# Lane pauses, layer-norm leads and one buffer ring in a hybrid encoder layer

## The chip, the cores and the metric

The kernel runs on one core of a Trainium2 chip. The metric is the device time of one execution in microseconds (us). Beside it stands the profiled execution, from which every duration below is taken: its span runs from the first instruction to the last.

The engines are named as in the profile: PE multiplies matrices, PEld loads its weights, DVE and ACT do elementwise work, POOL issues some transfers (DMAs), SP issues most of them. Each engine takes its instructions strictly in the order of the program.

## The reference

Two token sequences go through the same layer: a prompt of 512 tokens and a sample of 1024, both 2048 wide, in float32.

```
h    = rms_norm(x, norm_g)
z    = h @ w_in                      # 2048 -> conv value, GLU, gate, q, k, v, gate
conv = silu(layer_norm(depthwise31(val * sigmoid(glu)))) @ w_pw * silu(c_gate)
attn = banded_sink_attention(rope(q), rope(k), v) * silu(a_gate)   # 8 heads, 2 kv heads
y    = rms_norm(x + concat(conv, attn) @ w_out, final_norm_g)
```

The convolution is 1024 channels wide, with 31 taps. Attention goes by blocks of 128 queries, each over up to three blocks of 128 keys, with a sink logit for each head. The layer norm is over the 1024 convolution channels of one token.

## The kernel before

**Products.** Every operand of a large product is split into a high part (rounded by ACT) and a low part (the rest, by DVE); three matmuls, high by high, high by low and low by high, make one product. The sample's projections go through a Strassen-like scheme of seven products in place of eight (class Unit): a unit is a pair of output columns by half of the depth, seven products of 12 matmuls each, 84 in all. Weight sums are made by DVE (make1: `t2` is the second of them, the operand of product P6), token sums are loaded as they are wanted. The prompt's projection by w_in is plain: 44 jobs of 48 matmuls.

**Stages, in PE's order.** The sample's units on w_in; the prompt's 44 jobs; then the upper half of the depth of w_out for the sample (8 units), w_pw (4 units, class Gated), the lower half of w_out (8 units), and at the end the prompt's w_pw and w_out. Between two stages with other token sums stands a switch: the old stage's last unit and the new stage's first bring in the new sums, 4 tiles at a time (load_sum, token_sum). On the switch from w_pw to w_out's lower half the first two units run side by side, product by product: unit 0 in the PSUM banks a, b, c and unit 1 in s, s, pt. These two are of class Total.

**Lanes.** Everything that isn't a large product is written as generators in three lanes: attn, conv (the taps on DVE) and prep. After every three matmuls the main loop adds their nominal time times the lane's rate to its credit, and a lane with credit takes its next step. A generator says `yield n` to be left alone until n of credit is earned. So a yield divided by the rate is a distance on PE. The list of steps thus found goes through a scheduler that places every instruction in its engine's queue; what stands in the queues at the end is fixed when the program is built.

- `attention(g, b, k, v)` is one block of four heads: query parts, pause S1, scores (L1239) for two heads, pause S6, two more, pause S6, exponentials (L1253), S2, scaling by the reciprocal (L1258, L1260), S4, then for each key block transposes (L1273), parts, S5 and the product with V (L1268, bank pv).
- `group(g)` makes the parts of K and V and then runs the blocks. For the prompt these parts lie in the f ring of 7 buffers, which the taps, the sums and the layer norm share.
- The attn lane has rate 1.8 (RUSH) while the sample's attention starts, 2.2 from the prompt's job 18 on (prepare), and 2.0 (LATE) once `attention_sums` has multiplied the sample's attention by its gate and stored its sums. attention_sums goes in four steps j: load the heads (L1370 from att_d, L1371 from ag_d), pause, multiply (L1375), sums (L1354 to L1357) into the u and g rings, store. The prompt's two groups follow it in the lane.
- `Post.prepare` is the layer norm of one half of the sample's tokens, in the prep lane at rate 1.0: sums over channels, their spread over partitions by a product with ones (`sums`, L781), squares (L1616 to L1618), column sums (L769), reciprocal root (L787 to L792), diagonal matrices (`spread`, L805) and their product with ones (L810), then scaling. Between the operands and the product with ones stands a lead of S8 = 6000. LastPost is the same for the prompt, much later.

**Rings.** A tag is a ring of buffers; a new tile waits until an old one of its ring is read. Rings that matter here: a (4 buffers of 1024 columns: query parts, probability parts, wide token sums, gated attention), p (4 of 512: probabilities, narrow token sums), g and u (4 each of 512: PSUM copies and sums to be stored), f (7 of 1024).

**SP** issues loads and stores in the order of its queue, and a load that waits holds all behind it.

In class Unit the buffer of `t2` is chosen by these lines:

```
if self.late:
    t2 = self.e.G([HALF, P]) if self.side or not self.total else self.e.A([HALF, P], F32)
else:
    t2 = self.e.PT("p", NP, [HALF, P])
```

Of the kernel before, what the change touches and what calls it, by code (L numbers as in the profile page):

```python
# [22 lines left out]
NB = 4  # L23
# [70 lines left out]
class Unit:  # L94
# [34 lines left out]
    late = False  # L129
# [141 lines left out]
class Onto(Unit):  # L271


    late = True
# [38 lines left out]
class Gated(Unit):  # L313


    late = True
# [36 lines left out]
class Total(Unit):  # L353


    late = True
    next = None

    def __init__(self, e, w, cols, k, source, part, done):
# [137 lines left out]
class Encoder:  # L497
# [273 lines left out]
        nc.vector.tensor_scalar(v, ps[:, 0:b], mul, add, ALU.mult, ALU.add)  # L771
        return v

    def sums(self, x):

        hi, lo = self.U(dt=F32R), self.U(dt=F32R)
        self.parts(hi, lo, x)
        yield S8
        ps = self.PS("s", [W])
        for n, part in enumerate((hi, lo)):  # L780
            self.nc.tensor.matmul(ps, self.ones_r, part, start=n == 0, stop=n == 1)  # L781
        return ps
# [8 lines left out]
        nc.vector.tensor_scalar(t, t, -0.5, 1.5, ALU.mult, ALU.add)  # L791
        nc.vector.tensor_tensor(out, s, t, ALU.mult)  # L792

    def spread(self, cols, b=NB, room=None):

        nc = self.nc
        hi = self.work.tile([P, b], F32R, tag="tinyr", bufs=4, name=self.name("tinyr"))
        lo = self.small(b)
        nc.vector.tensor_copy(hi, cols)
        nc.vector.tensor_tensor(lo, cols, hi.bitcast(F32), ALU.subtract)  # L800
        parts = []
        for part in (hi.bitcast(F32), lo):
            dg = (room or self.U)([b * P], F32R)
            for j in range(b):
                nc.vector.tensor_scalar(dg[:, j * P : (j + 1) * P], self.ident, part[:, j : j + 1], None, ALU.mult)  # L805
            parts.append(dg)
        yield S8
        ps = self.PS("s", [b * P])
        for n, dg in enumerate(parts):
            nc.tensor.matmul(ps, self.ones_r, dg, start=n == 0, stop=n == 1)  # L810
        return ps


class Sequence:
# [407 lines left out]
    def attention(self, g, b, k, v):  # L1222

        e, nc, B = self.e, self.e.nc, self.B
        lo, hi = max(b - 1, 0), min(b + 2, B)
        n = (hi - lo) * P
        keys = slice(lo * P, hi * P)
        mask = e.mask[:, (lo - b + 1) * P : (hi - b + 1) * P]
        qs = e.A([2, GROUP, P])
        with e.tc.high_priority(SOON):  # L1230
            e.parts(qs[:, 0], qs[:, 1], self.q)
        self.load_query(g, b + 1)
        m, nm, es, l, r = (e.small(GROUP) for _ in range(5))
        yield S1
        pr = []
        for h in range(GROUP):
            ps = e.PS("s", [3 * P])
            for p, (x, y) in enumerate(((0, 0), (0, 1), (1, 0))):
                nc.tensor.matmul(ps[:, 0:n], qs[:, x, h], k[y][:, keys], start=p == 0, stop=p == 2)  # L1239
            p = e.PT("p", NP, [W])  # L1240
            with e.tc.high_priority(SOON):
                nc.vector.tensor_tensor_reduce(
                    p[:, 0:n], ps[:, 0:n], mask, SCALE, e.sink[:, g * GROUP + h : g * GROUP + h + 1],
                    ALU.add, ALU.max, accum_out=m[:, h : h + 1],
                )
            pr.append(p)
            if h % 2:
                yield S6
        with e.tc.high_priority(SOON):
            nc.vector.tensor_scalar(nm, m, -1.0, None, ALU.mult)  # L1250
            nc.vector.tensor_tensor(es, e.sink[:, g * GROUP : (g + 1) * GROUP], m, ALU.subtract)  # L1251
            for h, p in enumerate(pr):
                nc.scalar.activation(p[:, 0:n], p[:, 0:n], AF.Exp, bias=nm[:, h : h + 1], accum_out=l[:, h : h + 1])  # L1253
            nc.scalar.activation(es, es, AF.Exp)
        yield S2
        with e.tc.high_priority(SOON):
            nc.vector.tensor_tensor(l, l, es, ALU.add)
            nc.vector.reciprocal(r, l)  # L1258
            for h, p in enumerate(pr):
                nc.scalar.activation(p[:, 0:n], p[:, 0:n], AF.Identity, scale=r[:, h : h + 1])  # L1260
        yield S4
        pv = e.PS("pv", [GROUP, P])
        last = hi - lo - 1

        def products(i, pt):
            vs = slice((lo + i) * P, (lo + i + 1) * P)
            for p, (x, y) in enumerate(((0, 0), (0, 1), (1, 0))):
                nc.tensor.matmul(pv, v[x][:, vs], pt[:, y], start=i == 0 and p == 0, stop=i == last and p == 2)  # L1268

        for i in range(hi - lo):  # L1270
            tp = e.PS("pt", [GROUP, P])
            for h, p in enumerate(pr):
                nc.tensor.transpose(tp[:, h], p[:, i * P : (i + 1) * P], e.ident)  # L1273
            pt = e.A([2, GROUP, P])
            with e.tc.high_priority(SOON):
                e.parts(pt[:, 0], pt[:, 1], tp)
            yield S5
            products(i, pt)
        o = e.U([GROUP, P])
        with e.tc.high_priority(SOON):  # L1280
# [53 lines left out]
class Mix:  # L1334
# [26 lines left out]
    def attention_sums(self, then):  # L1361

        e, nc, seq = self.e, self.e.nc, self.seq
        for j in range(HALF):
            if j == HALF - 1:
                then()
            x = []
            for h in (j, j + HALF):
                f, g = e.A([TS], F32), e.F([TS])
                nc.sync.dma_start(f, seq.att_d[h // GROUP][:, h % GROUP, :])  # L1370
                nc.sync.dma_start(g, seq.ag_d[h])  # L1371
                x.append((h, f, g))
            yield e.attn.rate * 1.5 * LEAD
            for h, f, g in x:
                nc.vector.tensor_tensor(f, f, g, ALU.mult)  # L1375
                e.store(self.xT[NC + h], f)
                yield 1500
            self.block_sums(1, j, x[0][1], x[1][1])
            self.gated += 1
            yield 4000  # L1380
        e.attn.rate = LATE
# [197 lines left out]
class Post:  # L1579


    N = 512

    def __init__(self, e, seq, t0, out):
        self.e, self.seq, self.t0, self.out = e, seq, t0, out
# [2 lines left out]
    def prepare(self):  # L1588
        e, nc, seq, t0, N = self.e, self.e.nc, self.seq, self.t0, self.N
        cols = slice(t0, t0 + N)  # L1590
        bc, vs = self.room(), self.room()
        mu, rs, va = bc[:, 0], bc[:, 1], vs[:, 0]
        sq = (bc[:, 1], vs[:, 1])
        pairs = []
        for i in range(0, NC, 2):
            t = self.room()
            for j in (0, 1):
                nc.sync.dma_start(t[:, j], seq.conv_d[i + j][:, cols])
            pairs.append(t)
        xc = [pairs[i // 2][:, i % 2] for i in range(NC)]  # L1600
        both = lambda row: row.unsqueeze(1).broadcast_to([P, 2, N])
        yield 2 * LOAD
        nc.vector.tensor_tensor(vs, pairs[0], pairs[1], ALU.add)
        for t in pairs[2:]:
            nc.vector.tensor_tensor(vs, vs, t, ALU.add)
            yield 1500
        nc.vector.tensor_tensor(va, va, vs[:, 1], ALU.add)
        yield S3
        ps = yield from e.sums(va)
        nc.scalar.activation(mu, ps, AF.Copy, scale=1.0 / C)  # L1610
        yield 1000
        for i, t in enumerate(pairs):
            nc.vector.tensor_tensor(t, t, both(mu), ALU.subtract)
            for j in (0, 1):
                n = 2 * i + j
                nc.scalar.activation(sq[j] if n else va, t[:, j], AF.Square)  # L1616
                if n:
                    nc.vector.tensor_tensor(va, va, sq[j], ALU.add)  # L1618
            yield 2500
        yield S3  # L1620
        v = yield from e.column_sums(va, N, 1.0 / C, LN_EPS)
        r = e.small(NB)
        e.rsqrt(r, v, NB)
        yield S7
        ps = yield from e.spread(r)
# [12 lines left out]

# [21 lines left out]
class LastPost(Post):  # L1660


    PAIRS = (2, 3, 0, 1)
    HT = TP // 2

    def __init__(self, e, seq, t0, out, sums):
        super().__init__(e, seq, t0, out)
# [39 lines left out]
    def combine(self, m, x1, x2):  # L1707

        e, nc, h = self.e, self.e.nc, self.HT

# [584 lines left out]
```

## Time and profile before

| | |
|---|---|
| time, median of 3 | 2079.45 us (2077.16 to 2080.08) |
| the profiled execution's own time | 2082.61 us |
| its span | 2080.8 us |
| TensorE clock granted, mean | 0.997 |
| DVE busy | 1754.9 us (84%) |
| ACT busy | 1096.5 us (53%) |
| DMA, mean over the span | 237 GB/s |

A row of the groups of instructions or of the timeline names the line, the engine, the operation and the tiles written and read; "idle before" is how long that engine did nothing just ahead of it, with what ended the wait. PEclk is the TensorE clock that was granted, 1.00 at full speed. Matmul counts given below as places on PE are counts of the product matmuls of 512 columns (the projections' own) from the program's start; there are 8316.

### The profile page before, as it was taken

Reading aid. Unit: us, or ns where it says so; the run is one execution under the profiler, and the core shown is the slowest. Engines: PE = TensorE matmul, PEld = TensorE weight load, DVE = VectorE, ACT = ScalarE, POOL = GpSimd, SP = SyncE. Lnnn points to the kernel's source line nnn. Section 1 sums busy time; section 2 is a strip of 40 time slices with the busy share of each in tenths; the row PEclk is TensorE's granted clock in tenths of the full one; section 3 lists DMA queues with packets and bytes.
Section 4 is the critical chain, followed back from the end, with each engine's and each line's share of the span. In section 5 each row is a group of like instructions: output and inputs, shape, how many; then the busy total and the mean of one; then the engine's idle time right before and its main releaser. Section 6 shows DMA issues by size and latency. Waiting matters only on the chain.

```text
span 2080.8 us, 27254 instructions
## 1 busy us (share of the span) xinstructions
PE 2054.6 (99%) x9208; PEld 1685.7 (81%) x9208; DVE 1754.9 (84%) x2895; ACT 1096.5 (53%) x1811; POOL 160.8 (8%) x240
## 2 busy tenths in 40 slices
PE   9999999999999999999999999999999999999998
PEld 7888888888887888788888887878778887888886
DVE  8767899998899899879766888688998887998887
ACT  7485445333465555645555775358541544454554
POOL 0111111111111111100000000000001002100000
PEclk9999999999999999999999999999999999999999
DMA  8888886854577767854555567886899778778897
GB/s 288 309 300 256 197 218 227 300 205 153 194 240 194 179 168 180 276 166 157 162 184 175 162 204 246 305 281 220 254 306 345 242 256 247 243 255 287 287 329 278
DMA packets 245405, 492.99 MB, mean 237 GB/s; under 512 B 23952, under 2 KB 84752, under 8 KB 245264
## 3 DMA queue, kind: packets, MB, share of 16 engines
q1 hardware_dynamic: 218944, 427.26, 61.7%
q0 software_dynamic: 25024, 61.88, 12.5%
q10 hardware_dynamic: 1296, 2.11, 0.3%
q8 instruction: 72, 1.18, 0.2%
q14 instruction: 69, 0.57, 0.1%
HBM read 328.89 MB, written 162.27 MB: 236 GB/s over the span
## 4 chain that ended last, share of the span: by engine, by line
PE 72%; DMA 8%; DVE 8%; issue 7%; ACT 3%; POOL 1%; SPq 0%; ACTq 0%; POOLq 0%; DVEq 0%
PE a L207 22%; PE c L207 11%; PE a L736 10%; PE b L207 5%; PE b L736 5%; PE c L736 5%; PE a L1959 2%; PE pv L1268 2%; PE s L1239 2%; PE s L207 2%; DVE hl L577 1%; PE s L1959 1%; PE pt L1273 1%; DMA f<-ag_d 1%; DVE f L1073 1%
## 5 line engine op out<-in xcount | busy, mean ns | idle before, releaser
L207 PE MATMUL a<-t,hl 128*128 128x512 f32 x2832 | 683.0, 391 | 5.2 <-ACT hl L576 2.5
L207 PEld LDWEIGHTS a<-t,hl 128*128 128x128 f32 x2832 | 530.6, 188 | 118.7 <-ACT hl L576 3.3
L577 DVE TENSOR_TENSOR hl<-raw,hl 128x1024 fp32r<-128x1024 f32 (+3 forms) x334 | 333.8, 1000 | 147.4 <-ACT hl L576 146.0
L576 ACT ACTIVATE hl<-raw 128x1024 fp32r<-128x1024 f32 (+3 forms) x334 | 293.4, 879 | 296.9 <-PE c L207 83.8
L207 PE MATMUL c<-t,hl 128*128 128x512 f32 x1416 | 343.1, 390 | 1.3 <-ACT t L576 1.3
L207 PEld LDWEIGHTS c<-t,hl 128*128 128x128 f32 x1416 | 265.6, 188 | 57.0 <-ACT t L576 1.8
L736 PE MATMUL a<-t,hl 128*128 128x512 f32 x1152 | 287.0, 396 | 0.0
L736 PEld LDWEIGHTS a<-t,hl 128*128 128x128 f32 x1152 | 213.3, 189 | 42.4
L1110 DVE SCALAR_TENSOR_TENSOR f<-f,c_w_dw,f 128x512 f32<-128x512 f32 x248 | 173.1, 747 | 0.2
L207 PE MATMUL b<-t,hl 128*128 128x512 f32 x708 | 171.8, 390 | 0.0
L1073 DVE SCALAR_TENSOR_TENSOR f<-f,c_w_dw,f 128x512 f32<-128x512 f32 x232 | 162.6, 744 | 2.3 <-ACT f L1068 2.3
L207 PEld LDWEIGHTS b<-t,hl 128*128 128x128 f32 x708 | 132.6, 188 | 27.7 <-DVE t L577 0.4
L736 PE MATMUL c<-t,hl 128*128 128x512 f32 x576 | 143.5, 395 | 0.4 <-DVE hl L577 0.4
L736 PE MATMUL b<-t,hl 128*128 128x512 f32 x576 | 139.6, 393 | 1.8 <-DVE t L581 0.8
L736 PEld LDWEIGHTS b<-t,hl 128*128 128x128 f32 x576 | 106.8, 188 | 25.2 <-DVE t L581 1.1
L736 PEld LDWEIGHTS c<-t,hl 128*128 128x128 f32 x576 | 106.1, 188 | 21.7 <-DVE hl L577 0.8
L236 ACT ACTIVATE u<-a 128x512 f32<-128x512 f32 x89 | 53.0, 595 | 91.9 <-PE a L207 86.0
L236 ACT ACTIVATE g<-a 128x512 f32<-128x512 f32 x87 | 51.9, 596 | 89.2 <-PE a L207 81.3
L1102 DVE SCALAR_TENSOR_TENSOR f<-f,w_both,f 128x512 f32<-128x512 f32 x120 | 89.8, 749 | 2.0
L1253 ACT ACTIVATE p<-p,tiny 128x384 f32<-128x384 f32 (+1 forms) x96 | 54.6, 570 | 55.3 <-DVE tiny L1251 31.7
L576 ACT ACTIVATE a<-pt 128x512 fp32r<-128x512 f32 x64 | 37.9, 592 | 58.1 <-PE pt L1273 58.0
L577 DVE TENSOR_TENSOR a<-pt,a 128x512 fp32r<-128x512 f32 x64 | 43.9, 686 | 27.1 <-ACT a L576 26.8
(360 smaller groups left out, 2791.9 us busy)
## 6 DMA issues: line engine op xcount, KB each, us to landing
raw<-w_in SPq DMA_DIRECT2D x170, 512.0 KB, 5.2
raw<-w_out SPq DMA_DIRECT2D x31, 512.0 KB, 5.2
wsum_P<-raw SPq DMA_DIRECT2D x47, 256.0 KB, 3.5
raw<-wsum_P SPq DMA_DIRECT2D x18, 512.0 KB, 4.9
f<-x_s SPq DMA_DIRECT2D x16, 512.0 KB, 8.4
raw<-w_pw SPq DMA_DIRECT2D x16, 512.0 KB, 4.9
g<-wsum_P SPq DMA_DIRECT2D x28, 256.0 KB, 4.8
a<-sum_S SPq DMA_DIRECT2D x24, 256.0 KB, 6.2
```

The source lines that it names most:

```text
L207: nc.tensor.matmul(acc, hl[:, l, o, j, :], toks[j][:, r], start=name in FRESH and j == 0 and q == 0, stop=name in LAST and j == HALF - 1 a ...
L236: nc.scalar.activation(t, bank, AF.Copy)
L576: nc.scalar.activation(hi, x, AF.Copy)
L577: nc.vector.tensor_tensor(lo, x, hi.bitcast(F32), ALU.subtract)
L736: nc.tensor.matmul(job.acc[0], hl[:, l, kk // HALF, kk % HALF, :], r, start=i == 0 and p == 0, stop=i == nk - 1 and p == 2,)
L1073: nc.vector.scalar_tensor_tensor(t, h[:, j : j + T], w(j), t, ALU.mult, ALU.add)
L1102: nc.vector.scalar_tensor_tensor(m0, odd[:, j : j + H], both(j), m0, ALU.mult, ALU.add)
L1110: nc.vector.scalar_tensor_tensor(out, d[:, j : j + H], w(2 * j + k), out if j else m0, ALU.mult, ALU.add)
L1239: nc.tensor.matmul(ps[:, 0:n], qs[:, x, h], k[y][:, keys], start=p == 0, stop=p == 2)
L1253: nc.scalar.activation(p[:, 0:n], p[:, 0:n], AF.Exp, bias=nm[:, h : h + 1], accum_out=l[:, h : h + 1])
L1268: nc.tensor.matmul(pv, v[x][:, vs], pt[:, y], start=i == 0 and p == 0, stop=i == last and p == 2)
L1959: nc.tensor.matmul(acc[t], self.toks[name, m][:, x, i, t * P : (t + 1) * P], parts[i][l].rearrange("p a b -> p (a b)"), start=fresh and fi ...
```

## The change

Three things are edited.

1. In an attention block the pauses S6 and S4 are multiplied by `hurry`, the lane's rate over 1.8 and at least 1. At rate 2.2 that is 1.22, at 2.0 it is 1.11, at 1.8 nothing changes. The pause ahead of each multiplication of attention_sums grows from 1.5 to 2 times 9000 times the rate.
2. The layer norm of the sample's two halves gets 12000 in place of 6000 between operands and product with ones, at both places. The prompt's keeps 6000.
3. Class Total is no longer `late`: `t2` of the two switch units comes from the p ring. Before, unit 0's came from the a ring and unit 1's, which runs at the side, from the g ring.

```
 class Total(Unit):
-    late = True
     next = None
...
-    def sums(self, x):
+    def sums(self, x, lead=S8):
...
-        yield S8
+        yield lead
...
-    def spread(self, cols, b=NB, room=None):
+    def spread(self, cols, b=NB, room=None, lead=S8):
...
-        yield S8
+        yield lead
...
         m, nm, es, l, r = (e.small(GROUP) for _ in range(5))
+        hurry = max(1, e.attn.rate / RUSH)
         yield S1
...
             if h % 2:
-                yield S6
+                yield S6 * hurry
...
-        yield S4
+        yield S4 * hurry
         pv = e.PS("pv", [GROUP, P])
...
-            yield e.attn.rate * 1.5 * LEAD
+            yield e.attn.rate * 2 * LEAD
             for h, f, g in x:
                 nc.vector.tensor_tensor(f, f, g, ALU.mult)
...
 class Post:
     N = 512
+    lead = 2 * S8
...
-        ps = yield from e.sums(va)
+        ps = yield from e.sums(va, self.lead)
...
-        ps = yield from e.spread(r)
+        ps = yield from e.spread(r, lead=self.lead)
...
 class LastPost(Post):
     HT = TP // 2
+    lead = S8
```

No instruction of PE is added or taken away. From the middle of the sample's attention (place 4602) to the end of the prompt's, the queues of all engines are rearranged; the prompt's first scores move from place 5542 to 5631, its last product with V from 6159 to 6303. In the changed program lines between 358 and 1232 have numbers lower by one.

**DVE, the layer norm of the sample's second half.** Before, the rows from the reciprocal root (L788 to L792, tiles tiny) on; a_11176 and a_11180 are the first two heads of attention_sums, t_ tiles are the layer norm's. The diagonals L805 follow eight rows behind the last row shown.

```order
L788 RECIPROCAL tiny_11253<-tiny_11253 128x4
L1375 TENSOR_TENSOR a_11176<-a_11176,f_11177 128x1024
L789 TENSOR_TENSOR tiny_11254<-tiny_11253 128x4
L1073 SCALAR_TENSOR_TENSOR f_11109<-f_10957,c_w_dw,f_11109 128x512
L790 TENSOR_TENSOR tiny_11254<-tiny_11254,tiny_11250 128x4
L1375 TENSOR_TENSOR a_11180<-a_11180,f_11181 128x1024
L577 TENSOR_TENSOR hl_11360<-raw_11239,hl_11360 128x1024
L791 TENSOR_SCALAR tiny_11254<-tiny_11254 128x4
L1354 TENSOR_TENSOR u_11304<-a_11176,a_11180 128x512
L792 TENSOR_TENSOR tiny_11252<-tiny_11253,tiny_11254 128x4
```

With the change the same two multiplications (now of a_11221 and a_11225) stand among the sums of squares (L1619, into t_1493_10780), which PE's column sums read:

```order
L1375 TENSOR_TENSOR a_11221<-a_11221,f_11222 128x1024
L1619 TENSOR_TENSOR t_1493_10780<-t_1493_10780,t_1492_10779 128x512
L1375 TENSOR_TENSOR a_11225<-a_11225,f_11226 128x1024
L576 TENSOR_TENSOR hl_11306<-raw_11210,hl_11306 128x1024
L1619 TENSOR_TENSOR t_1493_10780<-t_1493_10780 128x512
L1072 SCALAR_TENSOR_TENSOR f_11054<-f_10925,c_w_dw,f_11054 128x512 x2
L1614 TENSOR_TENSOR t_1497_10790<-t_1497_10790,t_1492_10779 128x1024
L1072 SCALAR_TENSOR_TENSOR f_11054<-f_10925,c_w_dw,f_11054 128x512 x5
L1619 TENSOR_TENSOR t_1493_10780<-t_1493_10780,t_1492_10779 128x512
```

The multiplications moved from the far side of the column sums to the near side, twelve rows ahead of the first row that reads the column sums.

**DVE, the switch from w_pw to w_out.** Here a_15149 is t2 of unit 0, hl_15156 the parts made of it, t_ tiles are token parts. Before:

```order
L577 TENSOR_TENSOR t_2186_15064<-p_14967,t_2186_15064 128x512
L577 TENSOR_TENSOR t_2191_15089<-a_15005,t_2191_15089 128x512
L577 TENSOR_TENSOR t_2192_15092<-a_15005,t_2192_15092 128x512
L577 TENSOR_TENSOR t_2216_15221<-g_15076,t_2216_15221 128x512
L143 TENSOR_TENSOR a_15149<-raw_14985,raw_14882 128x512
L577 TENSOR_TENSOR t_2193_15095<-a_15006,t_2193_15095 128x512
L143 TENSOR_TENSOR raw_14882<-raw_14882,a_15149 128x512
L577 TENSOR_TENSOR hl_15156<-a_15149,hl_15156 128x512
```

With the change, p_15149 is t2 of unit 0 and p_15185 that of unit 1 (it was g_15185, 22 rows ahead of a_15149):

```order
L576 TENSOR_TENSOR t_2186_15064<-p_14967,t_2186_15064 128x512
L576 TENSOR_TENSOR t_2191_15089<-a_15005,t_2191_15089 128x512
L143 TENSOR_TENSOR p_15149<-raw_14985,raw_14882 128x512
L576 TENSOR_TENSOR t_2201_15134<-f_15132,t_2201_15134 128x512
L143 TENSOR_TENSOR raw_14882<-raw_14882,p_15149 128x512
L576 TENSOR_TENSOR t_2202_15139<-u_14940,t_2202_15139 128x512
L576 TENSOR_TENSOR t_2203_15142<-f_14971,t_2203_15142 128x512
L576 TENSOR_TENSOR hl_15156<-p_15149,hl_15156 128x512
L576 TENSOR_TENSOR t_2204_15146<-g_15014,t_2204_15146 128x512
L143 TENSOR_TENSOR p_15185<-f_15047,raw_14945 128x512
L257 TENSOR_TENSOR g_15210<-s_15224,g_15210 128x512
L143 TENSOR_TENSOR raw_14945<-raw_14945,p_15185 128x512
```

Unit 0's t2 is made nine rows earlier and unit 1's twenty rows later. p_15185 takes the buffer of p_15149 and waits until that tile's store to memory has landed. On PE, P6 of unit 0 now stands ahead of P6 of unit 1; before it stood behind it.

**ACT, K and V parts of the prompt's second group.** Before, K's part (f_12761) stood by itself, with V's (f_12762) eleven rows behind it:

```order
L576 ACTIVATE a_12920<-u_12767 128x512
L576 ACTIVATE t_1831_12850<-f_12805 128x512
L576 ACTIVATE hl_12976<-raw_12878 128x1024
L576 ACTIVATE f_12761<-a_12763 128x512
L576 ACTIVATE t_1854_12958<-f_12853 128x512
L576 ACTIVATE t_1855_12961<-f_12853 128x512
```

With the change both (f_13063, f_13064) stand together, and V's waits for the store of the taps' result (f_12420), whose buffer it takes:

```order
L575 ACTIVATE hl_13313<-raw_13156 128x1024
L575 ACTIVATE f_13063<-a_13065 128x512
L575 ACTIVATE f_13064<-a_13067 128x512
L575 ACTIVATE a_13179<-u_13069 128x512
L1067 ACTIVATE f_13195<-f_12998,c_b_dw,c_w_dw 128x512
L1068 ACTIVATE f_13195<-f_12998,c_w_dw 128x512
L575 ACTIVATE hl_13376<-raw_13156 128x512
```

They moved from the loading of the upper half's token sums (t_ tiles) into the units of w_out; weights for a unit (hl_13376) stand behind them.

More of the change, by code (lines that the diff above doesn't have):

```diff
@@ L353 @@
 class Total(Unit):
-    late = True
     next = None
@@ L772, in column_sums, with sums @@
         return v
-    def sums(self, x):
+    def sums(self, x, lead=S8):
         hi, lo = self.U(dt=F32R), self.U(dt=F32R)
         self.parts(hi, lo, x)
-        yield S8
+        yield lead
         ps = self.PS("s", [W])
@@ L792, in rsqrt, with spread @@
         nc.vector.tensor_tensor(out, s, t, ALU.mult)
-    def spread(self, cols, b=NB, room=None):
+    def spread(self, cols, b=NB, room=None, lead=S8):
         nc = self.nc
@@ L806, in spread @@
             parts.append(dg)
-        yield S8
+        yield lead
         ps = self.PS("s", [b * P])
@@ L1233, in attention @@
         m, nm, es, l, r = (e.small(GROUP) for _ in range(5))
+        hurry = max(1, e.attn.rate / RUSH)
         yield S1
@@ L1247, in attention @@
             if h % 2:
-                yield S6
+                yield S6 * hurry
         with e.tc.high_priority(SOON):
@@ L1260, in attention @@
                 nc.scalar.activation(p[:, 0:n], p[:, 0:n], AF.Identity, scale=r[:, h : h + 1])
-        yield S4
+        yield S4 * hurry
         pv = e.PS("pv", [GROUP, P])
@@ L1372, in attention_sums @@
                 x.append((h, f, g))
-            yield e.attn.rate * 1.5 * LEAD
+            yield e.attn.rate * 2 * LEAD
             for h, f, g in x:
@@ L1582 @@
     N = 512
+    lead = 2 * S8
     def __init__(self, e, seq, t0, out):
@@ L1608, in prepare @@
         yield S3
-        ps = yield from e.sums(va)
+        ps = yield from e.sums(va, self.lead)
         nc.scalar.activation(mu, ps, AF.Copy, scale=1.0 / C)
@@ L1624, in prepare @@
         yield S7
-        ps = yield from e.spread(r)
+        ps = yield from e.spread(r, lead=self.lead)
         nc.scalar.activation(rs, ps, AF.Copy)
@@ L1664 @@
     HT = TP // 2
+    lead = S8
     def __init__(self, e, seq, t0, out, sums):
```

## The prediction

> **What bounds the kernel now.** I read the page's first part first, then PE's waits, then windows round the longest of them.
>
> ```profile
> PE 2054.6 (99%) x9208; PEld 1685.7 (81%) x9208; DVE 1754.9 (84%) x2895; ACT 1096.5 (53%) x1811; POOL 160.8 (8%) x240
> ```
>
> PE sets the time. Of the span of 2080.8 us it is idle for 26.2, in the whole program. The change leaves PE's work as it is, so it can win only two things: idle time, and clock that idle time costs. PE's waits, grouped by the waiting line and its releaser (us in total, times, longest):
>
> ```profile
> PE s L810 <- DVE u L805: 2.5, 2, 2.3
> PE a L207 <- ACT hl L576: 2.5, 2, 2.0
> PE s L1239 <- ACT f L576: 1.5, 1, 1.5
> PE c L207 <- ACT t L576: 1.3, 1, 1.3
> PE a L207 <- DVE tiny L1258: 1.0, 1, 1.0
> ```
>
> The three longest belong to the three things that are edited: the layer norm's spread (L810), the switch's P6 (L207 on hl) and the prompt's first scores (L1239). Windows of 4 us behind each, and two long stretches (busy us and count of PE, PEld, DVE, ACT, POOL, then granted clock, DMA share, GB/s):
>
> ```profile
> 1294.00:1298.00 4.00, 3.63 (x10) 2.87 (x11) 4.00 (x11) 0.60 (x1) 0.00 (x0) 0.57 1.03 413
> 1374.00:1378.00 4.00, 3.02 (x18) 2.52 (x19) 3.92 (x10) 3.67 (x5) 0.00 (x0) 1.00 0.97 362
> 1436.00:1600.00 164.00, 162.01 (x749) 131.16 (x748) 156.85 (x282) 77.43 (x150) 14.83 (x27) 1.00 0.88 292
> 1734.00:1738.00 4.00, 3.78 (x11) 3.04 (x11) 4.00 (x7) 0.66 (x2) 0.00 (x0) 0.57 0.91 246
> 2000.00:2081.00 81.00, 70.65 (x311) 57.85 (x309) 59.30 (x110) 38.87 (x70) 0.00 (x0) 0.97 0.84 294
> ```
>
> Behind the first and third waits (2.32 and 2.00 us, below) the granted clock is 0.57; behind the second, of 1.5 us, it stays at 1.00. So a wait of 2 us or more costs a second time: 0.43 of 3.63 us is 1.6 us at the first, 0.43 of 3.78 is 1.6 us at the third. The last 81 us hold 10.35 us of the idle time, and the change doesn't reach them.
>
> (The Trainium skill, page "TensorE: Matmul & The Clock Gate", section "Why this matters for your kernels", advises only against idle gaps of more than about 3 us, which would make these waits free of clock; the two windows disagree, with 0.57 behind 2.32 and 2.00 us. By that rule the sum would lose its two clock terms; it is rival 2.)
>
> **Edit 2, the layer norm of the second half.** The chain of waits and the timeline at 1275 to 1295:
>
> ```profile
> 1275.61 6.41 DMA att_d<-u
> 1282.09 4.62 DMA a<-att_d
> ...
> 1293.54 0.80 DVE u L805 x4
> ...
> 1273.69 0.68 DVE L1618 TENSOR_TENSOR t<-t 128x512 f32<-128x512 f32 x1
> 1287.15 1.23 DVE L1375 TENSOR_TENSOR a<-a,f 128x1024 f32<-128x1024 f32 x1 [2.40 <-DMA a<-att_d]
> ...
> 1274.14 0.62 PE L1268 MATMUL pv<-a,t 128*128 128x512 f32 x2
> 1278.71 11.08 PE L736 MATMUL c<-t,hl 128*128 128x512 f32 x48
> 1294.37 0.79 PE L810 MATMUL s<-u,ones_r 128*128 128x512 f32 x1 [2.32 <-DVE u L805]
> ```
>
> DVE stood still for 2.40 us because a head that attention_sums multiplies was not back from memory; the diagonals L805 stood behind it, and PE waited 2.32 us for them. After the change the product with ones stands 76 product matmuls behind the column sums; by 11.08/48 = 0.231 us that is 17.5 us. The changed order has about 10 us of DVE rows between the two (0.6 us for a row of 512, 1.2 for one of 1024). Some 7 us are to spare: this wait goes, **-2.3 and -1.6 of clock**.
>
> What is late next: the same load now lies ahead of the column sums. By the row at 1274.14 the last product with V starts, 0.5 us later its result is copied, and 6.41 + 4.62 us of store and load follow. Counted from the end of DVE's last part for that product (0.6 us ahead of 1273.69), DVE's own rows up to the second multiplication fill 11.4 us and the load lands after 14.0, so DVE waits 2.6; 10.5 us of rows lead from there to the last sum of squares, at 24.5. PE reaches the column sums 95 matmuls behind its product with V, at 23.1. It waits 1.4 us with this store and load, and less with median ones:
>
> ```profile
> att_d<-u SPq DMA_DIRECT2D x24, 256.0 KB, 4.2
> a<-att_d SPq DMA_DIRECT2D x12, 512.0 KB, 6.1
> ```
>
> (KB, us to landing.) Together 10.3 against 11.03, so 0.7. I take **+1.0**; bounds 0 (both rows quicker by a microsecond) and 3.6 (2.0 of wait, and then clock). Column sums that wait hold all of PE's product matmuls behind them. The first half's longer lead lies in a stretch without a wait in the list: nothing.
>
> **Edit 1, the pauses.** The prompt's first scores, from the chain of waits:
>
> ```profile
> 1358.30 7.38 DMA f<-ag_d
> ...
> 1365.78 1.22 DVE a L1375
> ...
> 1368.54 3.97 issue
> ...
> 1374.40 0.53 ACT f L576
> ```
>
> A gate load of 7.38 us held DVE and through it K's part on ACT, which came 1.5 us too late for L1239. The pause in each of attention_sums' four steps grows by 0.5 x 9000 times the rate; divided by the rate that is 4.5 us of products, and the scores start 89 matmuls (20.6 us) later, while K's parts move less. I take the wait as gone, **-1.5**. The second group, though: V's part now waits for the store of the taps' result, and stands with K's ahead of scores that are placed 51 matmuls later than their lane asked for, so some wait is near. The store's row:
>
> ```profile
> conv_d<-f SPq DMA_DIRECT2D x8, 512.0 KB, 3.2
> ```
>
> A quarter of that is what I take, **+0.8**; bounds 0 and 3.8 (a 2.2 us wait and clock). Queued behind the waiting part on ACT are query parts and weights of the next unit.
>
> The pauses themselves (S6 = 2500 twice and S4 = 7000, 12000 ns together) put 12000 x 0.22 / 2.2 = 1.2 us of products, at rate 2.0 0.7 us, more into each block, where scores, exponentials, scaling and transposes follow one another. No row of PE's list for these blocks is above 1.0 us, so little can be gained there. The attention ends 144 matmuls (33 us) later, though, inside the units of w_out: six of its eight blocks lie there instead of four. The window 1436 to 1600, in which today's four lie, has 1.99 us of idle PE, 0.5 for a block; two more make 1.0, and by wider pauses less: **+0.7**; bounds -1 and +2.
>
> **Edit 3, the switch.** Timeline:
>
> ```profile
> 1714.52 0.68 DVE L1456 TENSOR_TENSOR f<-f,g 128x512 f32<-128x512 f32 x1
> 1724.76 0.50 PE L207 MATMUL c<-t,hl 128*128 128x512 f32 x1 [1.34 <-ACT t L576]
> 1731.88 0.68 DVE L143 TENSOR_TENSOR a<-raw,raw 128x512 f32<-128x512 f32 x1
> 1733.28 0.73 PE L207 MATMUL a<-t,hl 128*128 128x512 f32 x2 [2.00 <-ACT hl L576]
> 1734.23 0.65 PE L207 MATMUL pt<-t,hl 128*128 128x512 f32 x1 [0.22 <-ACT hl L576]
> ...
> wsum_P<-raw SPq DMA_DIRECT2D x47, 256.0 KB, 3.5
> ```
>
> Unit 0's t2 (the row at 1731.88) was made behind token parts that wait for loads; ACT rounded it, and PE waited 2.00 + 0.22 us. In the changed order it stands nine rows earlier, ahead of the rows that waited. Counted at 0.60 us a row from 1714.52 it is made at 1722.9, and its parts are ready at 1726.6; PE wants them 14 matmuls behind the row at 1724.76, at 1727.9. So **-2.2 and -1.6 of clock**. The wait of 1.34 us on a token part stays.
>
> What is late next: p_15185 takes p_15149's buffer. Its place in DVE's queue comes at 1727.2, the store of p_15149 lands at about 1727.5 (made at 1723.5, 3.5 us to landing, 0.5 to issue), then ACT's rounding, so PE's P6 of unit 1, due another 12 matmuls later at 1730.6, waits between 0 and 1.3 us: **+0.6**. Behind p_15185 on DVE stand rows that free PSUM banks; they are delayed by 0.3 us only, well inside PE's 9 us for two products.
>
> **Sum.** -3.9 + 1.0 - 1.5 + 0.8 + 0.7 - 3.8 + 0.6 = **-6.1 us**. The profiled execution took 2082.61, its span and 1.8 us round it; less 6.1 it is 2076.5. It lay 3.2 above the median of the three runs, so the median becomes 2079.45 - 6.1 = **2073.3 us**.
>
> **Rivals.** About 0.2% (4.2 us) is what a measurement of this kernel can tell from no change.
>
> 1. *New waits in place of the old.* Column sums wait 2.0 us and cost clock (3.6), K and V parts the same (3.8), P6 of unit 1 its 1.3: against -9.2 for what goes and +0.7 for blocks, that leaves +0.2. With one of the two, -3.4. For it: a load of 11 us is moved nearer to a wanted sum, not shortened. Against it: median rows give 0.7. Time 2076 to 2079.7, no change measured.
> 2. *No clock to win.* Were the 0.57 of these windows from something else than the waits, -3.0 would be left: 2076.4. The window at 1374, 1.5 us and 1.00, speaks against it.
> 3. *Slower: weights of w_out behind attention's stores.* Two more blocks lie in w_out's units, with their loads and stores in SP's queue between the loads of weights, and a load that waits there holds all behind it. The rows today:
>
> ```profile
> raw<-w_out SPq DMA_DIRECT2D x31, 512.0 KB, 5.2
> L143 DVE TENSOR_TENSOR raw<-raw,raw 128x512 f32<-128x512 f32 x59 | 40.4, 685 | 1.4 <-DMA raw<-w_out 1.0
> ```
>
> A unit is 84 matmuls, 19.4 us; its weights take 5.2, and DVE has waited for them 1.0 us in all. This decides only once an issue is held for some 10 us, as for a store of attention that waits on a late block. Three such units at 2.3 + 1.6 each make +11.7, less 6.1: +5.6, **2085 us**. One or two make 2077.2 or 2081.
>
> 4. *Nothing.* PE is 99% busy, and what the edits free is lost to the next row in the queues: 2079.
>
> **How the numbers follow.** The forecast, with what is near it, has 0.55; rival 1 has 0.22, rival 2 0.04, rival 3 0.15, rival 4 0.04. Low end: all three waits and their clock gone (-9.2), the 1.34 and the 1.0 of L1258 too, no new one: -11.5, **2068.0**. High end: the third rival with two held units and some of a third, **2082.5**; full three lie outside. Faster by over 0.2% holds the forecast, 0.55; same holds rivals 1, 2, 4, 0.30; slower 0.15.
>
> **What the changed profile would show.** Right: no wait of L810 on L805 and none of L207 on hl near 1730 above 1 us, granted clock of 0.95 or more in windows behind them; DVE's wait for a<-att_d ahead of the column sums, and at most 1.5 us of PE at L769; P6 of unit 0 ahead of unit 1's without a wait; L1239 without the 1.5; DVE's wait for raw<-w_out still about 1 us. Wrong: a window of 0.6 clock at a new place, L769 or L1239 with over 2 us, or raw<-w_out among PE's or DVE's longest releasers between 1460 and 1620.

## The result and the profile after

| | before | after |
|---|---|---|
| time, median of 20 | 2079.52 us (2074.95 to 2082.78) | 2075.07 us (2069.20 to 2078.09) |
| ratio, with its 95% interval | | 0.9979 (0.9972 to 0.9986) |
| profiled execution | 2082.61 us | 2072.63 us |

The kernel became 4.45 us faster; by the interval, 2.9 to 5.8 us. The two profiled executions differ by 10.0 us: one of them lies above its median, the other below. Two rows cannot be compared across them as if they were means; the experiments below each bring another profile, two of them of the changed kernel and one of the kernel before. Two slow executions, one of later_columns (5826.29 us) and one of without_hurry (9298.98 us), are left out of the ratios below.

The page's first part, of the changed kernel, and PE's waits (us in total, times, longest):

```profile
PE 2050.1 (99%) x9208; PEld 1685.0 (81%) x9208; DVE 1753.4 (85%) x2895; ACT 1100.6 (53%) x1814; POOL 160.5 (8%) x240
...
PE s L768 <- DVE t L1619: 1.8, 1, 1.8
...
PE s L1239 <- DVE tiny L1242: 1.1, 2, 0.9
PE pt L1273 <- ACT p L1260: 1.0, 2, 0.8
...
PE c L207 <- DVE t L576: 0.6, 1, 0.6
...
PE s L1239 <- DVE a L576: 0.5, 1, 0.5
...
PE s L809 <- DVE u L804: 0.2, 1, 0.2
```

The three longest waits of before are gone from the top. The spread's product (now L809) waits 0.2, P6 of the switch not at all. A new one stands first: the column sums (L768), 1.8 us.

The new wait, in the chain and the timeline of the changed kernel (DVE first, then PE):

```profile
1274.54 5.20 DMA att_d<-u
...
1279.80 5.79 DMA a<-att_d
...
1285.62 1.23 DVE L1375 TENSOR_TENSOR a<-a,f 128x1024 f32<-128x1024 f32 x1 [1.86 <-DMA a<-att_d]
1295.54 0.68 DVE L1619 TENSOR_TENSOR t<-t 128x512 f32<-128x512 f32 x1
...
1296.27 1.05 PE L768 MATMUL s<-ones,t 128*128 128x1 f32 x8 [1.85 <-DVE t L1619]
```

DVE waits for the same load as before, now ahead of the column sums. From the start of its second multiplication to the end of the last sum of squares pass 1296.2 - 1285.6 = 10.6 us; the prediction counted 10.5.

The switch in the changed kernel (DVE's t2 of units 0 and 1, then PE):

```profile
1718.11 0.68 DVE L143 TENSOR_TENSOR p<-raw,raw 128x512 f32<-128x512 f32 x1
...
1722.33 0.68 DVE L143 TENSOR_TENSOR p<-f,raw 128x512 f32<-128x512 f32 x1
...
1719.45 0.73 PE L207 MATMUL c<-t,hl 128*128 128x512 f32 x2 [0.58 <-DVE t L576]
...
1722.75 2.88 PE L207 MATMUL a<-t,hl 128*128 128x512 f32 x12
1725.47 2.88 PE L207 MATMUL s<-t,hl 128*128 128x512 f32 x12
```

P6 of unit 0 (bank a) and of unit 1 (bank s) run through without a wait, and the token part's wait (bank c) fell from 1.34 to 0.58.

Stretches of w_out with the prompt's blocks, in the changed kernel (PE's busy time first, the clock third from the end):

```profile
1436.00:1600.00 164.00, 163.18 (x763) 132.68 (x762) 155.46 (x289) 83.46 (x165) 15.91 (x29) 1.00 0.87 280
```

PE is idle there for 0.8 us; it was 2.0.

### The profile page after: what moved, and what is told of

Same layout as the page of the kernel before. It is cut to its first block, busy times and chain, and to the rows that moved or that the text cites. A ratio compares the mean times of both kernels' runs of the same rounds, so it can differ in the third digit from the quotient of the medians.

```text
span 2070.9 us, 27278 instructions
## 1 busy us (share of the span) xinstructions
PE 2050.1 (99%) x9208; PEld 1685.0 (81%) x9208; DVE 1753.4 (85%) x2895; ACT 1100.6 (53%) x1814; POOL 160.5 (8%) x240
## 4 chain that ended last, share of the span: by engine, by line
PE 82%; DVE 7%; DMA 6%; ACT 2%; issue 2%; SPq 0%; POOL 0%; ACTq 0%; DVEq 0%; POOLq 0%
PE a L207 27%; PE c L207 13%; PE a L735 10%; PE b L207 7%; PE b L735 6%; PE c L735 4%; PE a L1961 2%; PE pv L1268 2%; PE s L1239 2%; PE s L207 2%; PE s L1961 2%; PE pt L1273 1%; DVE hl L576 1%; DVE f L1072 1%; PE pt L207 1%
```

## The experiments

Each profile gives, beside its waits, the start on PE of every product matmul. Two stretches are compared throughout: products 4602 to 6600, in which edits 1 and 2 move instructions, and 6600 to 7200, in which edit 3 does. Ratios are to the kernel before on the same chip, with their 95% intervals. The runs below were timed in three groups, each on a chip of its own: after_again and the three single edits; without_ring, without_pause, without_lead and later_columns; before_again, earlier_loads, without_hurry and after_third. A line of the program can have a number one or two higher or lower from kernel to kernel (L768 is L769 elsewhere, L1273 is L1272 or L1274).

| kernel | edits | 4602 to 6600, us | 6600 to 7200, us | ratio |
|---|---|---|---|---|
| before | none | 545.8 | 143.7 | |
| before_again | none | 548.0 | 143.5 | |
| only_ring | 3 | 542.3 | 138.8 | 0.9988 (0.9978 to 0.9998) |
| only_lead | 2 | 544.3 | 142.9 | 0.9994 (0.9985 to 1.0004) |
| only_pause | 1 | 542.9 | 142.7 | 0.9987 (0.9977 to 0.9997) |
| without_ring | 1, 2 | 542.4 | 142.9 | 0.9989 (0.9980 to 0.9998) |
| without_pause | 2, 3 | 542.9 | 138.5 | 0.9977 (0.9967 to 0.9986) |
| without_lead | 1, 3 | 542.9 | 138.4 | 0.9964 (0.9951 to 0.9977) |
| the changed kernel | 1, 2, 3 | 541.8 | 139.3 | 0.9979 (0.9972 to 0.9986) |
| after_again | 1, 2, 3 | 543.5 | 139.4 | 0.9979 (0.9970 to 0.9988) |
| after_third | 1, 2, 3 | 543.9 | 139.3 | 0.9971 (0.9960 to 0.9982) |
| later_columns | 1, 2, 3 and a pause | 543.2 | 139.0 | 0.9974 (0.9963 to 0.9984) |
| without_hurry | half of 1, 3 | 542.2 | 140.0 | 0.9976 (0.9965 to 0.9988) |
| earlier_loads | 1 with 2.1, 3 | 552.1 | 139.9 | 1.0018 (1.0009 to 1.0028) |

Of before_again there is one execution alone, so no ratio.

**The scatter.** The changed kernel twice more, and the kernel before once more, both without an edit.

> The changed kernel once more, to see how much of the two profiles' difference (10.0 us, against 4.45 us of the medians) is scatter of single executions. Theory A (three waits gone, one come, each the same in every execution): the last product starts 8 to 9 us earlier than in the profile of before (2059.6 us), and the column sums' wait is 1.5 to 2.0 us without a half-clock window. Rival B (the size of the waits varies from run to run, since they end with a DMA): the last product starts anywhere between 2050 and 2056 us, and where the column sums wait over 2 us a half-clock window of 3.4 us follows. Time: both 2075, ratio 0.998.

> The changed kernel on the same chip as the three others. Theory A: 0.9979 to before again, slower than the kernel with earlier loads by 2 to 6 us; a wait of 1.8 to 2.0 us at the column sums. Rival: the differences between these kernels lie within their scatter, and both come out at 0.997.

> The kernel before, profiled once more, for the scatter of its waits: one profile of this code showed 2.3 us at L810 with a half-clock window behind it, another (edit 3 alone, the same code there) 0.7 us without one. Theory A (the row on which the prediction's largest term rests was at the long end of its scatter): products 4602 to 6600 take less than 545.8 us, between 542 and 545, and L810 waits under 2 us. Rival: 545.8 again with 2.3 us and a half-clock window. Products 6600 to 7200: 143 us by both.

The column sums waited 1.9 and 2.0 us in the two further profiles of the changed kernel: this wait is there every time. What it costs is not the same every time. The windows behind it, of the changed kernel's first profile and of after_again:

```profile
1298.00:1300.50 2.50, 2.50 (x12) 2.05 (x11) 2.50 (x4) 0.00 (x0) 0.00 (x0) 1.00 0.37 125
```

```profile
1298.00:1300.50 2.50, 2.50 (x7) 1.97 (x6) 2.50 (x5) 0.20 (x1) 0.00 (x0) 0.50 0.51 179
```

At the same code, 1.85 us of idle PE left the clock at 1.00 and 1.94 us brought it to 0.50, 7 matmuls in place of 12. The two profiles of the kernel before, and edit 3 alone (where this part of the code is that of before), show how far the spread's wait scatters. From before_again:

```profile
1284.08 1.22 DVE L1375 TENSOR_TENSOR a<-a,f 128x1024 f32<-128x1024 f32 x1 [2.03 <-DMA a<-att_d]
...
1291.31 0.50 PE L810 MATMUL s<-u,ones_r 128*128 128x512 f32 x1 [1.96 <-DVE u L805]
...
1373.41 0.50 PE L1239 MATMUL s<-f,a 128*128 128x256 f32 x2 [3.20 <-ACT f L576]
...
1375.00:1377.00 2.00, 2.00 (x9) 1.81 (x9) 1.53 (x5) 1.12 (x1) 0.00 (x0) 0.50 1.02 331
```

From only_ring:

```profile
1283.25 1.23 DVE L1374 TENSOR_TENSOR a<-a,f 128x1024 f32<-128x1024 f32 x1 [0.83 <-DMA a<-att_d]
...
1290.47 0.50 PE L809 MATMUL s<-u,ones_r 128*128 128x512 f32 x1 [0.75 <-DVE u L804]
```

The spread waits 2.3, 2.0 and 0.7 us, and it follows the store and load of the head that DVE multiplies: 6.41 + 4.62 = 11.0 us, 6.12 + 4.58 = 10.7 and 4.8 + 4.7 = 9.5, for which DVE waits 2.4, 2.0 and 0.8. The prompt's first scores wait 1.5, 3.2 and 1.1. By that, and by one, two and no half-clock windows, the stretch 4602 to 6600 takes 545.8, 548.0 or 542.3 us. Rival B of after_again holds here: these waits end with a DMA, and their size differs from run to run. Theory A holds for the size of the column sums' wait alone, not for its being free of a half-clock window. The rival of before_again, 545.8 with a row like the first, was nearer than theory A, since that profile came out longer still. Both theories of after_third missed: it came out at 0.9971, and the kernel with earlier loads 10 us behind it.

**Each edit alone.**

```
only_ring:   before, with   -    late = True     in class Total
only_lead:   before, with lead = 2 * S8 in sums and spread of class Post
only_pause:  before, with S6 * hurry, S4 * hurry, e.attn.rate * 2 * LEAD
```

> Edit 3 alone (class Total not late; pauses and leads as before). Theory A: the switch gives -4.4 us, as between the two profiles (2.2 us of wait on hl, 1.6 of clock, 0.7 of the token part's wait), so 2075.1 us, and the wait of 2.3 us at L810 and its half-clock window stay. Rival: the switch's wait in the profile of before was an unusually long one, and the median gains only 1 to 2 us: 2078.

> Edit 2 alone (doubled leads; pauses and ring as before). Theory A: the wait at the spread's product goes (-2.3, -1.6 of clock), the column sums wait some 1.5 us: -2.4 us, 2077.1 us; the prompt's first scores move from product 5542 to 5508 and wait 1.5 us or more. Rival: the wait only moves from the spread to the column sums, 2 us with clock: 2079.5 us, no change.

> Edit 1 alone (longer pauses; leads and ring as before). The spread's product stands 48 products behind the column sums in place of 60. Theory A: the prompt's first scores lose their wait (-1.5), but the spread's wait stays at 2 to 4 us with its half-clock window: 0 to +1, 2079 to 2080.5 us. Rival (the pauses are what brings the gain, and the load's wait of DVE lies elsewhere): -2 or more, 2077 us.

Edit 3 alone does in its stretch what it does in the whole change: 138.8 us, where five profiles with the old ring show 142.7 to 143.7 (mean 143.1) and nine with the new 138.4 to 140.0 (mean 139.2). That is -3.9 us. In each of the five with the old ring a half-clock window follows the switch's wait for hl, in none of the nine with the new. The shortest of the five waits, in only_lead:

```profile
1729.47 0.73 PE L207 MATMUL a<-t,hl 128*128 128x512 f32 x2 [1.49 <-ACT hl L576]
...
1731.00:1735.00 4.00, 4.00 (x12) 3.14 (x11) 3.71 (x6) 0.29 (x1) 0.00 (x0) 0.57 0.96 280
```

The ratio of edit 3 alone gives 0.12%, 2.5 us, with an interval from 0.4 to 4.6 that holds theory A's 4.4 and the rival's 1 to 2 alike. The spread's wait, which theory A let stay at 2.3 us, was 0.7 us, by the scatter shown above.

Edit 2 alone removes the spread's wait (0.2 us is left), and no wait at the column sums appears. Without edit 1 the last product with V of the sample's attention stands 130 products ahead of the column sums, in place of 95 in the changed kernel, and the head's store is issued 28.2 us ahead of the last sum of squares, in place of 21.0; so the load has landed when DVE comes to it. In its place two blocks wait 3.1 us at L1273. The ratio's 0.06% can't be told from nothing.

Edit 1 alone was the surprise, and theory A wrong: the spread's wait is gone without any change to the leads. DVE and PE in only_pause:

```profile
1279.78 1.22 DVE L1376 TENSOR_TENSOR a<-a,f 128x1024 f32<-128x1024 f32 x1
1280.98 0.67 DVE L805 TENSOR_SCALAR u<-c_ident,tinyr 128x128 fp32r<-128x128 f32 x3
...
1290.68 1.22 DVE L1376 TENSOR_TENSOR a<-a,f 128x1024 f32<-128x1024 f32 x1
...
1283.71 0.69 PE L810 MATMUL s<-u,ones_r 128*128 128x512 f32 x2
```

The longer pause in attention_sums has moved the second multiplication (at 1290.68), the one that waited for its load, behind the diagonals (L805), and there it waits no more; the first stands ahead of them and never waited. So edits 1 and 2 remove one and the same wait, in two ways. The ratio of 0.9987, 2.7 us, is the rival's.

**Two edits of three.**

```
without_ring:   after, with   +    late = True     in class Total
without_pause:  after, with S6, S4 and e.attn.rate * 1.5 * LEAD as before
without_lead:   after, with lead = S8 in class Post
```

> Edits 1 and 2, with class Total late as before. Product 6600 to 7200 takes 143 us with the old ring in three profiles (143.7, 142.9, 142.7) and 139 with the new (139.3, 139.4, 138.8). Theory A: 143 again, so 3.9 us slower than the changed kernel and the whole change's gain gone but for 0 to 1 us: ratio 0.9995 to 1.000, column sums waiting 1.9 us. Rival B (edits 1 and 2 carry half of the gain): ratio 0.9988 or less.

> Edits 2 and 3, without the longer pauses. Theory A (edit 2 alone removes the spread's wait too, without the column sums' new one, but its first scores stand at product 5508 and the blocks wait some 3 us at L1273 for the scaled probabilities): 139 us for products 6600 to 7200, L769 waits under 0.5 us, ratio to before 0.9975 to 0.998, as the changed kernel. Rival B (the pauses carry the gain): ratio 0.999.

> Edits 1 and 3, without the doubled leads. Theory A (edits 1 and 2 both take the gated attention's load out of the spread's way, and together they put it ahead of the column sums): with the short lead the multiplications L1375 stand behind the spread, neither L769 nor L810 waits, and the kernel is 1 to 2 us faster than the changed one: ratio to before 0.997 to 0.9975. Rival B (the doubled lead is what removes the spread's wait): L810 waits 2 us again, ratio 0.9990 or more.

without_ring shows the size of edit 3 in its stretch from the other side: 142.9 us, as theory A said, and a ratio of 0.9989. Its gain of 0.11% over before is edits 1 and 2 together, more than theory A allowed and 0.01% less than rival B asked for. By the ratios edit 3 is worth 0.12% alone and 0.10% as the difference of this kernel from the changed one; their intervals are too wide to tell that from the 3.9 us (0.19%) of the profiles.

without_lead has no wait at the column sums and 0.2 us at the spread, as theory A said, and the lowest ratio of all, 0.9964; but that is from six executions, and its interval overlaps that of the changed kernel. Its stretch 4602 to 6600 is no shorter (542.9 against 541.8 to 543.9), because another wait came in. PE's waits, the timeline and SP's waits of without_lead:

```profile
PE a L207 <- ACT t L575: 2.2, 1, 2.2
...
1458.11 0.69 DVE L576 TENSOR_TENSOR t<-f,t 128x512 fp32r<-128x512 f32 x1
1458.42 0.60 ACT L1281 ACTIVATE u<-pv 128x512 f32<-128x512 f32 x1 [1.03 <-PE pv L1268]
1458.87 0.81 SPq L947 DMA_DIRECT2D f<-mix_d  x2
1459.78 0.56 SPq L569 DMA_DIRECT2D att_d<-u  x1
1464.80 1.29 ACT L575 ACTIVATE t<-f 128x512 fp32r<-128x512 f32 x2 [3.66 <-DMA f<-mix_d]
1465.48 0.79 PE L207 MATMUL a<-t,hl 128*128 128x512 f32 x1 [2.19 <-ACT t L575]
...
SPq L947 <- DVE t L576: 4.7, 2, 2.6
```

The token part that PE waits for is made from a load (f<-mix_d) that SP issues at 1458.87, right after DVE has ended a token part that reads a buffer of the f ring (1458.80). The load stands in SP's queue ahead of the store of an attention block (att_d<-u), and it was issued before the copy of that block's product (u, L1281), which the chain of waits names as its releaser, ended at 1459.02. So neither that store nor that copy held it. only_pause shows the same 2.2 us at this place, later_columns below too, the changed kernel none. The doubled leads thus exchange a wait of 2.2 us here for one of 1.9 us there; on top of edit 1 they bring nothing that these runs can show.

without_pause has no wait at the column sums, as theory A said, but loses 3.0 us of PE at the blocks' transposes:

```profile
PE pt L1272 <- ACT p L1259: 3.0, 2, 2.0
```

In the changed kernel that group has 1.0 us. Its ratio is that of the changed kernel all the same: by these rows, what the pauses save at the blocks, the column sums' wait takes.

**The new wait taken away.** A pause ahead of the column sums of the sample's halves:

```
-        yield S3
+        yield S3 + (4000 if self.lead > S8 else 0)
         v = yield from e.column_sums(va, N, 1.0 / C, LN_EPS)
```

> The changed kernel with a pause of 4000 more ahead of the column sums of the sample's layer norm: they stand 25 products later (5247 for 5222), and the two multiplications that wait for a<-att_d stand behind the last sum of squares. Theory A: the column sums' wait of 1.9 us goes, DVE's wait for a<-att_d stays and costs nothing: 1.5 to 2 us faster than the changed kernel, ratio to before 0.997. Rival B (the wait moves on to the spread, L810, or the later end of the layer norm holds up w_pw's operands): no change against the changed kernel, 0.998.

The column sums don't wait any more, and others do:

```profile
PE a L207 <- ACT t L575: 2.2, 1, 2.2
PE s L1239 <- DVE tiny L1242: 2.1, 1, 2.1
PE pt L1273 <- ACT p L1260: 1.3, 1, 1.3
```

By the stretch, 543.2 us, nothing is gained: that is rival B, with other places than it named. The ratio of 0.9974 lies between the two theories and decides nothing. The token parts' wait is that of without_lead.

**Edit 1 taken apart.**

```
without_hurry:  edits 1 and 3, with hurry = 1
```

> Edit 3 and of edit 1 only the pause of attention_sums (2 x 9000); S6 and S4 as before, leads as before. Theory A (what helps of edit 1 is that the gated attention's multiplications move behind the spread): L810 waits under 0.5 us, ratio to before 0.997, as without leads. Rival B (the wider pauses in the blocks carry it: blocks wait at L1273 and L1239 without them): 1 to 2 us slower than that, 0.998.

The larger pause in attention_sums alone removes the spread's wait, as theory A said. Two waits at blocks stay:

```profile
PE s L1239 <- DVE tiny L1242: 2.1, 1, 2.1
PE pt L1273 <- ACT p L1260: 1.9, 1, 1.9
```

In the changed kernel they are 0.9 and 0.8 us, but in later_columns, with the same wider pauses S6 and S4, 2.1 and 1.3; at these two places it isn't shown that the pauses shorten them. No half-clock window followed either, so this profile is one of the shortest (542.2). The ratio of 0.9976 is rival B's within its interval and within theory A's; undecided.

**The held loads moved ahead.**

```
-            yield e.attn.rate * 2 * LEAD
+            yield e.attn.rate * 2.1 * LEAD     (and lead = S8)
```

> Edits 1 and 3 with 2.1 in place of 2 in the pause of attention_sums, and without the doubled leads. In SP's queue the last two loads f<-mix_d then stand ahead of the store att_d<-u of an attention block; with 2 they stand behind it, and PE waited 2.2 us at 1464 us for token parts made of them. Theory A (the store that waits for the block's product holds the loads): that wait goes with its half-clock window, up to 3.8 us faster than the kernel without leads: ratio to before 0.995 to 0.996. Rival B (the next loads behind the store are as late, or the blocks that move later wait in w_out): 0.9964 again or worse.

This one is slower than before, by 0.18%. PE no longer waits 2.2 us at the token parts, but the loads are late all the same: ACT waits for them, and PE for a block's part (a) that stands behind the token parts in ACT's queue. The loads do stand ahead of the store here, so the store was not what made them late, and theory A is wrong. The blocks also stand 18 products later and wait in new places. PE, DVE and ACT:

```profile
1393.51 0.50 PE L1239 MATMUL s<-f,a 128*128 128x256 f32 x2 [2.10 <-DVE a L576]
1452.94 0.73 PE L207 MATMUL a<-t,hl 128*128 128x512 f32 x2 [2.47 <-ACT hl L575]
1466.74 0.50 PE L1268 MATMUL pv<-a,f 128*128 128x512 f32 x1 [2.32 <-ACT a L575]
1506.04 4.58 PE L207 MATMUL a<-t,hl 128*128 128x512 f32 x12 [4.34 <-DVE u L304]
...
1505.20 0.69 DVE L304 TENSOR_TENSOR u<-a,u 128x512 f32<-128x512 f32 x1 [5.88 <-issue]
...
1463.26 0.63 ACT L575 ACTIVATE t<-f 128x512 fp32r<-128x512 f32 x1 [2.14 <-DMA f<-mix_d]
1464.90 1.31 ACT L575 ACTIVATE t<-f 128x512 fp32r<-128x512 f32 x2 [1.01 <-DMA f<-mix_d]
1466.11 0.58 ACT L575 ACTIVATE a<-pt 128x512 fp32r<-128x512 f32 x1
```

Four waits of 2 us or more make 11.2 us, and half-clock windows follow the first and the last. The profile doesn't name what held DVE for 5.88 us at 1505. A load of a tile u (u<-xT_s, issued by POOL), of the name that this row reads, starts at 1496.97 and takes 8.2 us, to 1505.1; that it was this load is likely, not shown.

## Why the prediction was right, point by point

- **The time.** 2073.3 us was forecast, 2075.07 measured, within the range and on the side forecast. The sum of -6.1 us is larger than the measured 4.45 and just outside that measurement's interval (2.9 to 5.8); after_third gave 0.29%, 6.0 us. Means of the profiles give -3.9 for the switch, and for products 4602 to 6600 545.4 (three profiles of before's code) less 543.1 (three of the changed kernel), -2.3; the three of before's code lie 5.7 us apart, so the -2.3 is rough.
- **Luck.** That the sum came near is in part luck. In the means of these profiles the spread's wait was worth 1.7 us and 1.1 of clock, and the column sums' wait, with its clock, cost 1.9 and 1.1. The two together, forecast at -2.9, come to about nothing. The first scores and the blocks, forecast at 0.0 together, gave about -1.8 (waits of 1.9 before and 1.3 after, 0.6 of clock, and 0.7 in the window of the blocks), and the switch gave 0.7 more than forecast.
- **The switch**, -3.8 + 0.6. Right in its mechanism, and -3.9 in place of -3.2: P6 of unit 1 had no wait at all, since t2 of unit 0 stood 4.2 us ahead of that of unit 1 (1718.11, 1722.33) and its store had landed. The token part's wait, which was to stay, fell by 0.76 between the first two profiles, but only by 0.3 in the means of the five with the old ring (1.0) and the nine with the new (0.7).
- **The spread**, -2.3 and -1.6 of clock. The wait goes, as forecast, but the credit was given to edit 2 alone: edit 1 alone removes it too. Its size, from one row, was at the long end: 2.3, 2.0 and 0.7 in three executions.
- **The column sums**, +1.0. The mechanism was right (DVE waits for a<-att_d 1.9 us, forecast 2.6, and 10.6 us of rows follow), the term was mis-sized: 1.8, 1.9 and 2.0 us, with a half-clock window behind two of the three. At most 1.5 us here was to be a sign that the prediction is right, and a window of 0.6 clock at a new place one that it is wrong. Taking less than the 1.4 us that the rows gave, because the median of the loads was shorter, was wrong: store and load took 11.0, 11.1 and 11.1 us in the three profiles of the changed kernel, not 10.3.
- **The first scores**, -1.5 + 0.8. In the changed kernel 1.4 us are left at the scores: 0.5 at the first, behind query parts, not K's, and 0.9 at the next, behind DVE's row maxima (L1242). Before, the first scores waited 1.5, 3.2 and 1.1. The second group's V part, for which the 0.8 stood, shows no wait.
- **Two more blocks in w_out**, +0.7. Wrong in sign: 0.8, 1.3 and 1.0 us of idle PE in 1436 to 1600 in the three profiles of the changed kernel, 2.0, 1.4 and 1.7 in the three of before's code. The prediction said that the wider pauses had little to gain at the blocks. In this window, the token parts' wait of 2.2 us aside, seven profiles with the wider pauses have 0.8 to 1.5 us of idle PE and the six without 1.4 to 3.0; earlier_loads, with its new waits, has 9.1.
- **Rival 1**, new waits in place of the old, is what happened between edits 1 and 2: its price for the column sums, 2.0 us and clock, is what two of three profiles show. Its other two waits, at K and V parts and at P6 of unit 1, did not come.
- **Rival 2**, that the waits cost no clock, falls: edit 3 gains 3.9 us in its stretch, where waits of 2.2 us go and with them a window of 0.50 clock that all five profiles with the old ring have and none with the new. (The Trainium skill, page "TensorE: Matmul & The Clock Gate", section "Why this matters for your kernels", advises against idle gaps of more than about 3 us; here gaps of 1.9 to 2.0 us were followed by a clock of 0.50 in some executions.)
- **Rival 3**, weights of w_out held in SP's queue behind attention's stores, doesn't show in the changed kernel: DVE waits for raw<-w_out 2.4 us in all in place of 1.0, but none of it between 1460 and 1620. A wait of 2.2 us for token parts does come in without_lead, only_pause and later_columns, by a load that stood ahead of the store. The changed kernel happens to be without it.
- **Slips in the working.** Rival 2's sum is -2.9 and 2076.5, not -3.0 and 2076.4. Two products of 12 matmuls take PE 5.6 us (1722.75 to 1728.35 in the switch above), not 9. Neither moved the forecast.

## What to carry to other kernels

Where a kernel keeps its main engine at 99%, what is left are a handful of waits of about 2 us, each the end of a chain through the queues; a change of distances removes one and makes another nearby, so ask of each moved instruction not only what it no longer holds up but what it holds up now. Two edits that were made for different waits may remove the same one, and then their gains don't add: run each alone. And a wait that ends with a DMA can scatter as widely as its own size (0.7 to 2.3 us here, 1.1 to 3.2 at another place); three profiles of the same code say more than the longest row of one. Where the chain of waits puts a load down to an instruction, look in the timeline whether that instruction had ended when the load was issued.

## What was not expected of the hardware

Half clock after a short idle time isn't certain. In the stretch from 1120 to 1800 us of the fourteen profiles, PE stood idle for 1.8 us or more 22 times; 14 of these were followed by a window of 0.50 clock, which the trace's record of the clock gives 3.4 us each time (1.7 us lost), and 8 were not, among them waits of 2.47 and 2.32 us. One more window followed a wait of 1.49 us (only_lead), while 1.54 us in the kernel before had none. So in these profiles the length of the wait alone doesn't tell, between 1.5 and 2.5 us. The same wait of the changed kernel went both ways: 1.85 us without a window, 1.94 and 2.0 us with one. By these numbers each such wait can make two executions of one kernel differ by 1.7 us.
